# A decoder layer in one kernel: gates in column tiles, 1/rms columns by transfer, and three stretches in another order

## The chip, the core and the metric
The kernel runs on one core of a Trainium2 chip. The metric is the device time of one execution in microseconds (us). TensorE (PE) multiplies, VectorE (DVE), ScalarE (ACT) and GpSimd (POOL) work element by element, and SyncE (SP) issues most transfers. Each engine works through its own instructions in order and waits for others by semaphores.

## The reference
One step of a hybrid decoder layer for a prompt of 1024 tokens and 8 sequences of 8 new tokens, 1088 columns in all, in fp32:

```python
def rmsnorm(x, g):
    y = xf * lax.rsqrt(jnp.mean(xf * xf, axis=-1, keepdims=True) + EPS)
    return y * g

h = rmsnorm(x, pre_mix_g)
proj = h @ w_in               # 8 heads' q, k, v, output gate; 8 gate columns
i_pre, f_pre = gates          # + bias: 4 input and 4 forget gates
q_r, k_r = rotary(q_r, pos), rotary(k_r, pos) * scale
ret_out, S_new = retention_chunked(q_r, k_r, v_r, S_ret)            # 4 heads
ml_out, C, n, m = mlstm_chunked(q_m, k_m * scale, v_m, i_pre, f_pre, C, n, m)
ret_y = head_groupnorm(ret_out, ret_g) * silu(g_r)
ml_y = head_groupnorm(ml_out, ml_g) * sigmoid(o_m)
x = x + rmsnorm(concat([ret_y, ml_y]) @ w_out, post_mix_g)

up = rmsnorm(x, pre_ffn_g) @ w_up                # 1024 -> 2 x 2816
conv = causal depthwise convolution of width 3 over up, + conv_b
ffn = (gelu(gate) * value) @ w_down              # 2816 -> 1024
x = x + rmsnorm(ffn, post_ffn_g)
```

## The kernel before
Features lie on the 128 partitions and tokens on the free axis, in four blocks of 272 (`BLK`, `Q`). A large matmul is made of three fp32r products: each operand is split into a high part (a copy on ACT, L148) and a low part (a subtraction on DVE, L150), and `product` (L164) multiplies high by high, low by high and high by low. A projection (`proj`) loads and splits a weight of 128 columns and runs, block by block, 8 k-tiles x 3 products of 128x272; `proj`'s evacuation functions take each result from PSUM. What is multiplied there is x times the norm's gain; 1/rms of the token (`rb`, the same on all partitions) is multiplied in at the evacuation, for q and k of the retention heads through the rotation tables (L308).

The stages that the change touches:

- **Start of the mixer.** v of heads r0 and r1, then q of r0 with `pre_norm` in its middle, which sums squares on PE (`ssqb_pm`, L213) and forms `rb` block by block (L214 to L220), then k of r0. `token_norms` turns `rb` into columns (`rcol`, tokens on partitions) by matmuls with a column of the identity (L332). `gate_proj` projects the 8 gates: it splits the gates' weight and puts high and low side by side in 64 + 64 columns, so that each of the four blocks takes 8 x 2 matmuls (L359), evacuated by ACT and DVE. Four projections of output gates (12 to 15) follow, then head r0.
- **Gate tables.** `gate_consts` loads tables for the mLSTM heads (`xst`, from which DVE makes `upb` and `negsb`; `xsel`, which ACT copies to `sel`, L379). It stands behind head r0.
- **Heads.** `mix_head` goes through chunks of 128 tokens in pairs, `pair_of`, and the decode samples at last, `sample`. Every four chunks, and behind the sample, `finish` normalises the outputs on DVE (`on`, L687) and transposes them on PE (`yt`, L689) into `yT`. At a head's end two such `finish` are due: chunks 4 to 7 (four transposes) and the sample (one). The scheduler places their transposes among the matmuls of the next head's first projection.
- **FFN.** Of 22 pairs of up-projections (j), the first two (`PLAIN`) are multiplied directly and the others by a Strassen scheme with seven products on a pool of eight PSUM banks (psF); each product has two halves of 12 matmuls (L1088 to L1090), one bank each. Its operands T1 to T4 are differences of blocks of the input, split once. At the first Strassen pair (j = 2) there stand side by side: these splits, the weights' splits, the convolutions (`conv`, L1101 and L1103), gelu (L1107) and products (`pair_out`) of the plain pairs, and the evacuation of the first products: A11 by ACT (L1073), the others by DVE (L1062, L1066).

What sets the order is the order of the code, refined by a scheduler within each engine, and `tc.issue_after`, which holds an instruction back until a given one has been issued. PSUM pools have 2 banks (psA) and 6 banks (psB) in the mixer; a tile of a pool waits until the earlier tile in its place has been read.

## Time and profile before
| | before |
|---|---|
| time, median of 3 runs | 1339.77 us (1339.24 to 1342.83) |
| the profiled execution | 1338.16 us, of which the profile's span is 1336.4 us |
| mean granted clock of TensorE | 0.995 |
| PE busy | 1313.4 us, 98% of the span |
| DVE, ACT, POOL busy | 76%, 45%, 32% |

The profile is of one execution; "busy" excludes the issuing of transfers. The chain is followed back from the last instruction, each time to what released it. In it and in the rows of waits, a name such as `up_S` is a tile, and L1088 a line of the kernel. A matmul's own duration in the trace overlaps the next one's; what one costs is read from the distance of two starts, or from a piece of the chain.

### The profile page before, as it was taken

Reading aid. Unit: us, or ns where it says so; the run is one execution under the profiler, and the core shown is the slowest. Engines: PE = TensorE matmul, PEld = TensorE weight load, DVE = VectorE, ACT = ScalarE, POOL = GpSimd, SP = SyncE. Lnnn points to the kernel's source line nnn. Section 1 sums busy time; section 2 is a strip of 40 time slices with the busy share of each in tenths; the row PEclk is TensorE's granted clock in tenths of the full one; section 3 lists DMA queues with packets and bytes.
Section 4 is the critical chain, followed back from the end, with each engine's and each line's share of the span. In section 5 each row is a group of like instructions: output and inputs, shape, how many; then the busy total and the mean of one; then the engine's idle time right before and its main releaser. Section 6 shows DMA issues by size and latency. Waiting matters only on the chain.

```text
span 1336.4 us, 26898 instructions
## 1 busy us (share of the span) xinstructions
PE 1313.4 (98%) x10563; PEld 1301.6 (97%) x10563; DVE 1011.2 (76%) x2038; ACT 604.7 (45%) x1158; POOL 433.3 (32%) x565
## 2 busy tenths in 40 slices
PE   9999999999999999999989999999999999999996
PEld 9999999999999999999989999999999999999995
DVE  7877976558567467577899887877878788995677
ACT  7544433213324336455564443343434455463563
POOL 0344431589764000001144212222122214962002
PEclk9999999999999999999999999999999999999998
DMA  6433441576884214224034434433344359533363
GB/s 241 129 124 127 164 152 64 176 232 223 215 185 145 62 51 172 76 95 137 32 122 165 137 117 146 151 132 129 120 146 139 130 190 328 170 97 96 94 218 134
DMA packets 92734, 192.58 MB, mean 144 GB/s; under 512 B 16192, under 2 KB 41408, under 8 KB 92096
## 3 DMA queue, kind: packets, MB, share of 16 engines
q1 hardware_dynamic: 80304, 148.80, 33.6%
q0 software_dynamic: 12160, 41.95, 10.3%
q8 instruction: 83, 1.36, 0.4%
q14 instruction: 43, 0.35, 0.1%
q10 hardware_dynamic: 144, 0.11, 0.0%
HBM read 134.36 MB, written 56.47 MB: 143 GB/s over the span
## 4 chain that ended last, share of the span: by engine, by line
PE 92%; DVE 5%; ACT 1%; DMA 1%; issue 1%; SPq 0%; DVEq 0%; ACTq 0%
PE in L164 27%; PE out L164 7%; PE up_S L1090 6%; PE up_S L1088 6%; PE up_S L1089 6%; PE dn L1299 5%; PE dn L1300 5%; PE dn L1301 5%; PE up_A L1089 5%; PE up_A L1088 4%; PE up_A L1090 4%; PE up_A L1135 1%; PE up_A L1136 1%; PE up_A L1134 1%; PE gates L359 1%
## 5 line engine op out<-in xcount | busy, mean ns | idle before, releaser
L164 PE MATMUL in<-hh,wh_in 128*128 128x272 f32 x1024 | 297.8, 293 | 2.2 <-ACT wh_in L148 1.3
L164 PE MATMUL in<-hh,wl_in 128*128 128x272 f32 x1024 | 297.0, 292 | 0.0
L164 PE MATMUL in<-hl,wh_in 128*128 128x272 f32 x1024 | 296.9, 292 | 0.0
L164 PEld LDWEIGHTS in<-hh,wh_in 128*128 128x128 f32 x1024 | 192.4, 188 | 4.2 <-ACT wh_in L148 1.8
L164 PEld LDWEIGHTS in<-hl,wh_in 128*128 128x128 f32 x1024 | 192.0, 188 | 1.9 <-issue 1.7
L164 PEld LDWEIGHTS in<-hh,wl_in 128*128 128x128 f32 x1024 | 192.5, 189 | 0.1
L148 ACT ACTIVATE wh_up<-st_up 128x1024 fp32r<-128x1024 f32 x84 | 80.4, 959 | 163.4 <-PE up_S L1089 90.5
L150 DVE TENSOR_TENSOR wl_up<-st_up,wh_up 128x1024 fp32r<-128x1024 f32 x84 | 98.2, 1171 | 8.8 <-ACT wh_up L148 8.8
L1062 DVE TENSOR_TENSOR Uv<-Uv,up_S 128x272 f32<-128x272 f32 (+1 forms) x200 | 66.3, 375 | 46.1 <-PE up_S L1090 46.0
L1228 DVE TENSOR_TENSOR rb<-rb 128x544 fp32r<-128x544 f32 x78 | 75.0, 967 | 33.7 <-ACT rb L1227 33.3
L1227 ACT ACTIVATE rb<-rb 128x544 fp32r<-128x544 f32 x78 | 50.5, 650 | 77.2 <-DMA rb<-bd 65.3
L1248 POOL TENSOR_TENSOR wd<-wd 128x512 f32<-128x512 f32 x44 | 74.6, 1724 | 32.0 <-issue 12.7
L794 POOL TENSOR_TENSOR tab<-tab 128x256 f32<-128x256 f32 x104 | 80.5, 784 | 8.9 <-DMA tab<-in_wu 4.4
L1120 POOL TENSOR_TENSOR act<-act 128x544 f32<-128x544 f32 x40 | 64.4, 1610 | 57.6 <-DMA bd<-act 38.3
L1103 DVE SCALAR_TENSOR_TENSOR c<-Uv,vec,c 128x1024 f32<-128x1024 f32 (+1 forms) x88 | 69.0, 788 | 9.6 <-ACT c L1101 9.6
L1053 POOL MEMSET Ug<- 128x2 f32 x22 | 2.2, 100 | 217.2 <-DMA xr<-in_x 106.2
L1103 DVE SCALAR_TENSOR_TENSOR c<-Ug,vec,c 128x1024 f32<-128x1024 f32 x88 | 67.7, 805 | 0.0
L794 POOL TENSOR_TENSOR wq<-wq 128x256 f32<-128x256 f32 x56 | 49.7, 899 | 49.1 <-DMA wq<-in_wu 46.9
L1101 ACT ACTIVATE c<-Ug,vec 128x1024 f32<-128x1024 f32 (+1 forms) x44 | 34.6, 834 | 51.4 <-DVE Ug L1066 47.3
L794 POOL DMA_DIRECT2D tab<-in_wu x52 | 36.9, 715 | 51.4 <-DVE k_r L510 36.8
L150 DVE TENSOR_TENSOR wl_in<-st_in,wh_in 128x1024 fp32r<-128x1024 f32 (+2 forms) x33 | 40.7, 1233 | 13.8 <-ACT wh_in L148 13.8
L1088 PE MATMUL up_S<-B3h,wh_up 128*128 128x272 f32 x160 | 46.9, 293 | 3.7 <-ACT Uv L1073 3.7
(575 smaller groups left out, 4629.5 us busy)
## 6 DMA issues: line engine op xcount, KB each, us to landing
rb<-bd SPq DMA_DIRECT2D x76, 272.0 KB, 2.9
st_up<-sd SPq DMA_DIRECT2D x40, 512.0 KB, 3.8
bd<-act SPq DMA_DIRECT2D x33, 544.0 KB, 4.3
st_in<-in_wi SPq DMA_DIRECT2D x31, 512.0 KB, 4.4
tab<-in_wu POOLq DMA_DIRECT2D x52, 256.0 KB, 5.0
sd<-tab POOLq DMA_DIRECT2D x26, 512.0 KB, 3.9
st_up<-in_wu SPq DMA_DIRECT2D x24, 512.0 KB, 3.4
wd<-in_wd SPq DMA_DIRECT2D x44, 256.0 KB, 4.5
```

Of the source, the lines that this page charges most:

```text
L148: act = nc.scalar.activation(hi, x, AF.Copy)
L150: last["split"] = act, eng.tensor_tensor(lo, x, hi.bitcast(F32), ALU.subtract)
L164: nc.tensor.matmul(ps, u[:, k * P:(k + 1) * P], x[b // 2][k // 4][v][:, k % 4, qcols(b)], start=k == term == 0, stop=k == KT - 1 and term ...
L794: last["sums"] = f(*args)
L1088: nc.tensor.matmul(ps, wh[:, c], xh[:, k, n], start=k == 0, stop=False)
L1089: nc.tensor.matmul(ps, wh[:, c], xl[:, k, n], start=False, stop=False)
L1090: nc.tensor.matmul(ps, wl[:, c], xh[:, k, n], start=False, stop=k == 3)
L1103: nc.vector.scalar_tensor_tensor(c, u(i), cw(i), c, ALU.mult, ALU.add)
L1228: nc.vector.tensor_tensor(lo, x, hi.bitcast(F32), ALU.subtract)
L1248: nc.gpsimd.tensor_tensor(quad(p, out), quad(p, x), quad(p, y), op)
L1299: nc.tensor.matmul(t, wh[:, ms], ah, start=k == 0, stop=False)
L1300: nc.tensor.matmul(t, wh[:, ms], al, start=False, stop=False)
```

## The change
Five edits at once.

1. **Gates in column tiles.** The gates' weight is no longer split. DVE multiplies the eight used columns by the norm's gain in fp32; 32 fp32 matmuls with 32 columns each follow (8 k-tiles x 4 blocks, the blocks inside), each block into 32 partitions of its own in one bank. They multiply x itself (`xs`). Four DVE multiplies by `rb` evacuate the bank, and a transfer moves the input gates to their partitions.
2. **1/rms columns by transfers.** `token_norms` writes one row of `rb` to memory (`rbd`) and reads it back with tokens on partitions: one transfer for the eight chunks and four for the samples. The 9 matmuls (18 records, two passes each) go.
3. **Gate tables behind the gates.** `gate_consts` is called behind `gate_proj`, not behind head r0.
4. **Heads' ends.** A head's last two `finish` are kept in `held_back` and run in the next head's projections, with the transposes held back until k's block 3 (chunks 4 to 7) and v's block 0 (sample) have been issued.
5. **First Strassen pair.** T3's difference and splits now come before T1's, the convolutions of plain pair 0 wait for these splits, and gelu, products and the second plain pair's convolutions are issued behind product A11, with gelu held back until A11's evacuation (`last["evac"]`).

The order of PE's instructions at the gates, before (`in_3` is the last block of r0's k, `hh`, `hl` the high and low parts of the input):

```order
L164 MATMUL in_3_744<-hl_192,wh_in_647 128x272
L332 MATMUL rcol<-cst,rb 128x1 x2
L332 MATMUL rcol<-cst,sp_rb 128x1
L359 MATMUL gates_797<-hh_146,w_gates 128x272
L359 MATMUL gates_797<-hl_147,w_gates 128x272
```
And after (`in_1_887` is a block of projection 12, `x_102` to `x_105` the four token blocks of x):

```order
L164 MATMUL in_1_887<-hl_149,wh_in_854 128x272
L356 MATMUL gates<-x_102,st_gates 32x272
L356 MATMUL gates<-x_103,st_gates 32x272
L356 MATMUL gates<-x_104,st_gates 32x272
L356 MATMUL gates<-x_105,st_gates 32x272
```
Neighbours now belong to different blocks, and 18 matmuls of projection 12 stand ahead of the gates, between and behind the blocks of k.

ACT's order ahead of the gates, before (`sw_kr` are the swapped halves of k's blocks; `in_1`, `in_2` their banks):

```order
L508 ACTIVATE sw_kr_707<-in_1_682 64x272
L509 ACTIVATE sw_kr_707<-in_1_682 64x272
L508 ACTIVATE sw_kr_738<-in_2_713 64x272
L509 ACTIVATE sw_kr_738<-in_2_713 64x272
L508 ACTIVATE sw_kr_769<-in_3_744 64x272
```
And after:

```order
L509 ACTIVATE sw_kr_708<-in_1_683 64x272
L510 ACTIVATE sw_kr_708<-in_1_683 64x272
L380 ACTIVATE sel<-xsel 100x1024
L509 ACTIVATE sw_kr_739<-in_2_714 64x272
L510 ACTIVATE sw_kr_739<-in_2_714 64x272
```
The copy of `sel` stands ahead of block 2's swaps. On DVE the gain multiplies (L352), `upb` and `negsb` stand right behind the first block's L215, and on SP the load of `xsel` stands behind `rbd`, which reads the finished `rb`.

PE's order at the end of head m0, before (`on_m`, `on_m0s`: the head's normalised outputs; `in_3`: a block of the next head's first projection):

```order
L689 MATMUL yt_m_4219<-cst,on_m_4064 128x128
L164 MATMUL in_3_4457<-hh_189,wl_in_4376 128x272
L689 MATMUL yt_m_4219<-cst,on_m_4064 128x128
L164 MATMUL in_3_4457<-hl_190,wh_in_4375 128x272
L164 MATMUL in_3_4457<-hh_191,wh_in_4375 128x272
```
The other two transposes of `yt_m` stand just ahead of these rows, and `yt_m0s` follows five matmuls behind the last one shown. And after (`in_3_4348` is k's block 3, `in_0_4409` v's block 0):

```order
L164 MATMUL in_3_4348<-hh_191,wh_in_4266 128x272
L164 MATMUL in_3_4348<-hh_191,wl_in_4267 128x272
L164 MATMUL in_3_4348<-hl_192,wh_in_4266 128x272
L699 MATMUL yt_m_4393<-cst,on_m_4007 128x128 x4
L164 MATMUL in_0_4409<-hh_146,wh_in_4405 128x272
```
The four transposes stand together behind k's last block; `yt_m0s` stands behind v's four blocks, 96 matmuls later.

ACT's order at the first Strassen pair, before (`Uv<-up_A` on L1073: A11's two banks):

```order
L148 ACTIVATE wh_up_0_8586<-st_up_0_8584 128x1024
L148 ACTIVATE wh_up_1_8649<-st_up_1_8647 128x1024
L1107 ACT_TABLE_LOAD
L1107 ACTIVATE c_8504<-c_8504 128x1088
L1073 ACTIVATE Uv_8577<-up_A_8426 128x272
L1073 ACTIVATE Uv_8577<-up_A_8439 128x272
```
And after:

```order
L148 ACTIVATE wh_up_0_8529<-st_up_0_8527 128x1024
L1086 ACTIVATE Uv_8492<-up_A_8369 128x272
L1086 ACTIVATE Uv_8492<-up_A_8382 128x272
L1119 ACT_TABLE_LOAD
L1119 ACTIVATE c_8453<-c_8453 128x1088
L148 ACTIVATE wh_up_1_8592<-st_up_1_8590 128x1024
```
A11's evacuation moved ahead of the table load, the gelu and a weight's copy. On DVE, T3's splits moved ahead of T1's, and the next weight's second split behind A12's evacuation and `act`.

The diff:

```diff
@@ -161 +161 @@
     def product(ps, w, x, b, k, term):
 
         u, v = ((w[0], 0), (w[1], 0), (w[0], 1))[term]
-        nc.tensor.matmul(ps, u[:, k * P:(k + 1) * P], x[b // 2][k // 4][v][:, k % 4, qcols(b)],
-                         start=k == term == 0, stop=k == KT - 1 and term == 2)
+        last["product", b] = nc.tensor.matmul(ps, u[:, k * P:(k + 1) * P], x[b // 2][k // 4][v][:, k % 4, qcols(b)],
+                                              start=k == term == 0, stop=k == KT - 1 and term == 2)
 
     def dense(ps, w, x, b):
 
@@ -325 +325 @@
     def spread_tile(name):
         return m2.tile([P, NB * 129], F32, tag="vx", bufs=1, name=name)
 
+    rbd = dr.tile([1, T], F32, name="rbd")
+
     def token_norms():
-        ps = bank(psB, 9, "rcol")
-        rs = spread_copy(rb, spread_tile("sp_rb")[:, :P])
-        for c in range(9):
-            nc.tensor.matmul(ps[:, c:c + 1], chunk(rb, c) if c < 8 else rs, ident[:, 0:1], start=True, stop=True)
-        nc.vector.tensor_copy(rcol, ps)
+        nc.sync.dma_start(rbd, rb[0:1, :])
+        nc.sync.dma_start(rcol[:, :NCH], rbd[0, :LP].rearrange("(c p) -> p c", p=P))
+        for g in range(G):
+            nc.sync.dma_start(rcol[GW * g:GW * (g + 1), NCH:], rbd[0, LP - LEAD + TS // G * g:][:GW].unsqueeze(1))
 
 
     idb = mp.tile([P, P], BF16, name="idb")
@@ -345 +346 @@
     gates = []
 
     def gate_proj():
-        fg = yT[3][32:32 + NH, 0, :]
-        ig = yT[3][:NH, 0, :]
+        w = stage_w(a["wg"], "gates").rearrange("p (k c) -> p k c", k=KT)
+        gain = vec[:, V_PREMIX:V_PREMIX + KT].unsqueeze(2).broadcast_to([P, KT, NH])
+        for c in range(2):
+            nc.vector.tensor_tensor(w[:, :, NH * c:NH * (c + 1)], w[:, :, 32 * c:32 * c + NH], gain, ALU.mult)
+        ps = bank(psA, Q, "gates")
+        for k in range(KT):
+            for b in range(4):
+                nc.tensor.matmul(ps[GW * b:GW * (b + 1), :], w[:, k, :GW], xs[b][:, k, :],
+                                 start=k == 0, stop=k == KT - 1)
+        yT.extend(flat("yT", i, k=2) for i in range(4))
+        both = yT[3][:2 * NH, 0, :]
+        fg, ig = yT[3][:NH, 0, :], yT[3][32:32 + NH, 0, :]
         gates.extend([fg, ig])
-        st = stage_w(a["wg"], "gates").rearrange("p (k c) -> p k c", k=KT)
-        w = wp.tile([P, D], F32R, tag="whi", name="w_gates").rearrange("p (k c) -> p k c", k=KT)
-        split_to(st[:, :, :64], w[:, :, :64], w[:, :, 64:])
         for b in range(4):
             o0, n = BLK[b]
-            ps = bank(psA, n, f"gates{b}")
-            for k in range(KT):
-                for i, x in enumerate(h[b // 2][k // 4]):
-                    nc.tensor.matmul(ps, w[:, k, :], x[:, k % 4, qcols(b)], start=k == i == 0,
-                                     stop=k == KT - 1 and i == 1)
-            gs = m2.tile([P, Q], F32, tag="sw", name=f"gs{b}")[:64, :n]
-            nc.scalar.activation(gs, ps[64:, :], AF.Copy)
-            nc.vector.tensor_tensor(gs, gs, ps[:64, :], ALU.add)
-            nc.vector.tensor_tensor(fg[:, o0:o0 + n], gs[0:NH, :], rb[0:NH, o0:o0 + n], ALU.mult)
-            nc.vector.tensor_tensor(ig[:, o0:o0 + n], gs[32:32 + NH, :], rb[32:32 + NH, o0:o0 + n], ALU.mult)
+            own = slice(GW * b, GW * b + 2 * NH)
+            nc.vector.tensor_tensor(both[:, o0:o0 + n], ps[own, :], rb[own, o0:o0 + n], ALU.mult)
+        nc.sync.dma_start(ig, yT[3][NH:2 * NH, 0, :])
         nc.scalar.activation(fg, fg, AF.Identity, bias=vec[0:NH, V_BG:V_BG + 1])
         nc.scalar.activation(ig, ig, AF.Identity, bias=vec[0:NH, V_BG + 1:V_BG + 2])
 
@@ -538 +539 @@
 
     EARLY = (0, 1, 2, 3)
     turns = {"wq": 0}
-    early = []
+    early, held_back = [], []
+
+    def finish_previous(n, b):
+        for _ in range(min(n, len(held_back))):
+            held_back.pop(0)(last["product", b])
 
     def mix_head(hd, ml):
 
@@ -555 +560 @@
         if ml:
             proj((16 + hd, evac_norm(q, 1.0)))
             proj((20 + hd, evac_norm(k, SCALE)))
+            finish_previous(1, 3)
             proj((24 + hd, evac_copy(v)))
+            finish_previous(1, 0)
         else:
             eq, ek = evac_rot(q, f"q{nm}"), evac_rot(k, f"k{nm}")
             if hd == 0:
@@ -564 +571 @@
             else:
                 proj((hd, eq))
                 proj((NH + hd, ek))
+                finish_previous(1 if hd > 1 else 2, 3)
             if hd == 0:
                 token_norms()
-                yT.extend(flat("yT", i, k=2) for i in range(4))
             if hd > 1:
                 proj((2 * NH + hd, evac_copy(v)))
+                finish_previous(1, 0)
             if hd == 0:
                 gate_proj()
+                gate_consts()
                 for _ in range(5):
                     next(rows)
                 for i in range(NH):
@@ -662 +671 @@
...
-        def finish(on, mv, c0, L, name):
+        def finish(on, mv, c0, L, name, after=None):
 
             sh = [P, L]
             small = lambda tag: m2.tile([P, 4], F32, tag=tag, name=f"{tag}_{name}")[:, :L]
@@ -686 +695 @@
             for i in range(L):
                 nc.vector.tensor_scalar(on[:, i, :P], on[:, i, :P], mv[:, i, 0:1], A[:, i:i + 1],
                                         ALU.subtract, ALU.mult)
-                nc.tensor.transpose(ps[:, i * P:(i + 1) * P], on[:, i, :P], ident)
+                with tc.issue_after(after.ins) if after else nullcontext():
+                    nc.tensor.transpose(ps[:, i * P:(i + 1) * P], on[:, i, :P], ident)
             y = yT[hid // 2][:, hid % 2, c0 * CH:c0 * CH + L * P if c0 < 8 else T]
...
@@ -728 +738 @@
             nc.sync.dma_start(o["cs" if ml else "ss"][hd].rearrange("p (s v) -> p s v", s=NB), sb[:, :, :P])
...
-            return lambda: finish(on, mv, 8, 1, f"{nm}s")
+            return lambda after=None: finish(on, mv, 8, 1, f"{nm}s", after)
 
         S = None
         g = math.exp(CH * LG[hd])
@@ -761 +771 @@
                 S = S2
             stats(on, po, c0 % 4, 2, mv, f"{nm}{c0}")
             if c0 % 4 == 2:
-                return lambda: finish(on, mv, c0 - 2, 4, f"{nm}{c0}")
+                return lambda after=None: finish(on, mv, c0 - 2, 4, f"{nm}{c0}", after)
 
         todo = None
         order = [[0, 1], [2, 3], [4, 5], [6, 7], [8]]
@@ -769 +779 @@
         for i, cs in enumerate(order):
             cur, ready = ready, front(order[i + 1]) if i + 1 < len(order) else None
             done = sample(*cur) if cs == [8] else pair_of(cs[0], *cur)
-            if todo:
+            if todo and i + 1 == len(order) and hid + 1 < 2 * NH:
+                held_back.append(todo)
+            elif todo:
                 todo()
             todo = done
             next(rows, None)
             if hid > 2 or i % 2 == 0:
                 next(wsums, None)
         nc.sync.dma_start(o["cp" if ml else "sp"][hd], S)
-        todo()
+        if hid + 1 < 2 * NH:
+            held_back.append(todo)
+        else:
+            todo()
 
 
     sd = dr.tile([JT, P, 4, D // 2], F32, name="sd")
@@ -824 +839 @@
     rows = gate_rows()
     for hd in range(NH):
         mix_head(hd, False)
-        if hd == 0:
-            gate_consts()
...
@@ -1070 +1083 @@
...
-            "A11": ("B1", lambda i, ps: nc.scalar.activation(first(i), ps, AF.Copy)),
+            "A11": ("B1", lambda i, ps: last.update(evac=nc.scalar.activation(first(i), ps, AF.Copy))),
...
@@ -1100 +1113 @@
         for c, u in ((C[:, :LP], lambda i: U[:, i:i + LP]), (seq(C[:, LP:]), lambda i: own[:, :, i:i + LS])):
             nc.scalar.activation(c, u(2), AF.Identity, scale=cw(2), bias=vec[:, V_CB + jt:V_CB + jt + 1])
             for i in (1, 0):
-                nc.vector.scalar_tensor_tensor(c, u(i), cw(i), c, ALU.mult, ALU.add)
+                last["conv"] = nc.vector.scalar_tensor_tensor(c, u(i), cw(i), c, ALU.mult, ALU.add)
+
+    def gelu():
+        last["gelu"] = nc.scalar.activation(cs_[:, 0, :], cs_[:, 0, :], AF.Gelu_apprx_tanh)
 
     def convs(j, ug, uv):
         conv(ug, cs_[:, 0, :], j)
-        last["gelu"] = nc.scalar.activation(cs_[:, 0, :], cs_[:, 0, :], AF.Gelu_apprx_tanh)
+        gelu()
         conv(uv, cs_[:, 1, :], JT + j)
 
     def pair_out(j):
@@ -1173 +1189 @@
             split(name, i, sums[name][:, :, qcols(i)])
 
     difference("T2", 4)
+    last["sq"], last["acc"] = last["split"]
+    difference("T3", 6)
+    last["sq"], last["acc"] = last["split"]
     difference("T1", 10)
     last["sq"], last["acc"] = last["split"]
     next(prep)
     cs_ = flat("c", 3, k=2)
-    convs(0, *firsts[0][2])
-    difference("T3", 6)
+    for c, u in enumerate(firsts[0][2]):
+        conv(u, cs_[:, c, :], JT * c)
+    last["acc"] = last["conv"]
     for _ in prep:
         pass
     X["T4"] = [bigp.tile([P, 4, 2 * Q], F32R, tag=f"f{i}", name=f"T4{'hl'[i]}") for i in range(2)]
     for i in range(2):
         split("T4", i, mo[1][0][:, :, qcols(i)])
     acts_ = flat("act", 2, k=2)
-    for j, _, rows in firsts:
-        if j:
-            convs(j, *rows)
-        pair_out(j)
+
+    def finish_plain():
+        with tc.issue_after(last["evac"].ins):
+            gelu()
+        pair_out(0)
+        convs(1, *firsts[1][2])
+        pair_out(1)
+
     for j in range(PLAIN, JT):
         ws = nxt
         prep = weight_prep(j + 1) if j + 1 < JT else iter(())
@@ -1199 +1223 @@
             for name in names:
                 for i in range(2):
                     (held.pop(0) if held else product(name, i))()
+                if j == PLAIN and name == "A11":
+                    finish_plain()
             nxt = next(prep, None) or nxt
         convs(j, ug, uv)
         pair_out(j)
```

## The prediction
> **What bounds the kernel now.** I read the page's busy times and its chain first, then PE's waits, then chain, timelines and clock around each wait that the change touches.
>
> ```profile
> PE 1313.4 (98%) x10563; PEld 1301.6 (97%) x10563; DVE 1011.2 (76%) x2038; ACT 604.7 (45%) x1158; POOL 433.3 (32%) x565
> PE 92%; DVE 5%; ACT 1%; DMA 1%; issue 1%; SPq 0%; DVEq 0%; ACTq 0%
> ```
> PE is busy for 98% of the span and carries 92% of the chain that ended last. Time is won by issuing less to PE or by taking one of its few stalls away. Of the view of PE's waits three rows bear on the change (who waited for whom; us in total, times, longest):
>
> ```profile
> PE up_S L1088 <- ACT Uv L1073: 3.7, 1, 3.7
> ...
> PE in L164 <- DVE k_r L510: 0.9, 1, 0.9
> ...
> PE yt_m L689 <- DVE on_m L687: 0.7, 3, 0.3
> ```
>
> **Gates and 1/rms columns.** The chain near the start (start, us, what):
>
> ```profile
> 34.42 0.46 PE ssqb_pm L213 x2
> ...
> 54.23 1.23 PE rcol L332 x12
> 55.46 6.15 PE in L164 x48
> 61.61 0.56 PE rcol L332 x6
> 62.17 4.12 PE gates L359 x32
> 66.29 1.63 PE in L164 x13
> 67.92 4.01 PE gates L359 x32
> ```
> Before, the gates are 64 matmuls of 272 columns: 4.12 + 4.01 = 8.1 us. After, they are 32 fp32 matmuls, each on 32 of the array's 128 columns. What an fp32 matmul of 272 columns costs shows ssqb_pm: two passes (x2), 0.46 us. One behind the other, 32 of them cost 32 x 0.46 = 14.7 us; four neighbours side by side, 8 x 0.46 = 3.7 us. The order puts the four token blocks inside the loop over k, so neighbours sit on different column tiles. Which price holds, the decode samples' product tells; it has the same tiling:
>
> ```profile
> 328.89 0.65 PE L706 MATMUL o_m<-sb_m,qx 128*32 128x129 f32 x16
> 329.46 0.72 PE L717 MATMUL us_m<-sp_m,kz_m 32*128 32x258 f32 x8
> ```
> These 16 records are 8 fp32 matmuls on 32 columns, two passes each; from their start to the next instruction's it is 329.46 - 328.89 = 0.57 us. A pass of 272 columns is 0.23 us, so one of 129 should be 0.23 x 129/272 = 0.109: 16 in a row would need 1.74 us, four at a time 0.44. The group is near the second, with 0.13 left for the change of tiling. Each tile there reads its own moving data and loads its own weights, as the gates' tiles will. I take 3.7 + 0.1 = 3.8 us: **-4.3 us** (ends: -4.5, and +6.6 without overlap).
>
> The Trainium skill, "TensorE: Matmul & The Clock Gate", Part 3: Packing small matmuls, reports 2.38x for three column tiles, a share of 0.79 of the full factor. By that the gates would take an estimated 3.7/0.79 = 4.7 us, and the sum would be 0.9 us higher. The trace's own factor is 1.74/0.57 = 3.05 of four, about that share, but over a stretch so short that the switch of tiling weighs in it.
>
> The 18 rcol records leave PE: 1.23 + 0.56 = **-1.8 us**. In their place SP's queue gets one transfer of rb to memory and five of 4-byte elements back. The nearest row (last column: us from issue to landing):
>
> ```profile
> sb_m<-in_sn SPq DMA_DIRECT2D x4, 4.0 KB, 5.8
> ```
> Two such steps take some 12 us; rcol's first reader is head r0's front, behind the gates and four output-gate projections (4 x 96 matmuls of 0.128 = 49 us). Head r0's state and the following weight loads stand behind them in the queue, under the same cover. I cost them at nothing (ends 0 and +2); without the cover, r0's front would wait.
> The gates' evacuation (four DVE multiplies on 8 partitions for four ACT copies and twelve DVE operations) lies beside PE's projections: nothing.
>
> **Gate tables.** Before, they are loaded behind head r0 and stop DVE, then PE:
>
> ```profile
> 147.99 3.08 DMA xst<-in_cx
> ...
> 151.09 0.75 DVE upb L375
> ```
> ```profile
> 151.91 0.29 PE L164 MATMUL in<-hl,wh_in 128*128 128x272 f32 x1
> 153.06 0.39 PE L164 MATMUL in<-hh,wh_in 128*128 128x272 f32 x1 [0.86 <-DVE k_r L510]
> ```
> From 151.91 to 153.06 it is 1.15 us where 0.13 is usual: **-1.0 us** (other end 0, if DVE is late there anyway). Now the new place. ACT's copy to sel waited long for its transfer, and DVE's rows of the start say when the tables would come:
>
> ```profile
> 157.00 1.06 ACT L379 ACTIVATE sel<-xsel 100x1024 fp32r<-100x1024 f32 x1 [3.69 <-DMA xsel<-in_cx]
> ```
> ```profile
> 35.27 0.36 SPq L136 DMA_DIRECT2D st_gates<-in_wg  x1
> ```
> ```profile
> 38.46 0.43 DVE L215 TENSOR_SCALAR rb<-ssqb_pm 128x272 f32<-128x272 f32 x1
> ...
> 46.29 0.44 DVE L218 SCALAR_TENSOR_TENSOR sums_sb<-sums_sb,rb 128x272 f32<-128x272 f32 x1 [0.68 <-ACT sums_sb L217]
> ...
> 52.47 0.44 DVE L220 SCALAR_TENSOR_TENSOR rb<-sums_sb 128x272 f32<-128x272 f32 x1
> ```
> ```profile
> 58.63 0.40 ACT L508 ACTIVATE sw_kr<-in 64x272 f32<-64x272 f32 x1 [2.22 <-PE in L164]
> ```
> Behind the first L215 (38.46), DVE now needs st_gates, issued at 35.27, and xst, issued behind it (3.1 us): it goes on at about 40.3 instead of 38.8, 1.5 late. Of that, 0.7 goes into the idle time at 46.29; PE's banks are ahead there, nothing lost. The last block's 1/rms (52.47) then comes 0.8 later, and about 1.3 more since proj 12's weight split and two k_r operations now stand ahead of it: 54.5, done 54.9. SP waits for it with rbd, then issues xsel: 55.5, landed 3.6 later at 59.1. ACT copies sel (1.06) to 60.2, and only then does the swaps of k's block 2, which stood at 58.63; with these (0.8) and DVE's read (0.4), k's bank is free at 61.4. The gates need it at 62.17 - 1.8 (rcol) + 18 x 0.128 (matmuls of projection 12 that now stand ahead) = 62.7. So 1.3 us are left: **0** (ends 0 and +2).
>
> **Heads' ends.** The transposes that wait at the ends of m0 and m1:
>
> ```profile
> 337.37 0.33 PE L689 MATMUL yt_m<-cst,on_m 128*128 128x128 f32 x1 [0.32 <-DVE on_m L687]
> ...
> 339.10 0.30 PE L689 MATMUL yt_m0s<-cst,on_m0s 128*128 128x128 f32 x1 [0.29 <-DVE on_m0s L687]
> ```
> ```profile
> 389.24 0.30 PE L689 MATMUL yt_m1s<-cst,on_m1s 128*128 128x128 f32 x1 [0.42 <-DVE on_m1s L687]
> ```
> 0.32 + 0.29 + 0.42 = 1.03 us idle, and 0.16 each for the start after it (k_r's stall: 1.02 lost, 0.86 of it idle): **-1.5 us** (other end 0). The change holds the transposes back by at least a projection (24 matmuls, 3 us, or more), over twice the longest wait. The other two waits of yt_m (0.7 in all) are inside a head, and stay. What is late next: yT, which only the output projection reads, far later.
>
> **First Strassen pair.**
>
> ```profile
> 673.67 0.29 PE L1090 MATMUL up_S<-T1h,wl_up 128*128 128x272 f32 x1
> 677.69 0.39 PE L1088 MATMUL up_S<-B3h,wh_up 128*128 128x272 f32 x1 [3.73 <-ACT Uv L1073]
> ```
> ```profile
> 673.87 1.06 ACT wh_up L148
> 674.95 1.28 ACT L1107
> ...
> 677.26 0.39 ACT Uv L1073
> ```
> ```profile
> 677.69:681.65 3.96, 3.96 (x20) 0.58 0.46 133
> 681.65:685.60 3.95, 3.95 (x33) 0.99 0.53 202
> ```
> PE has filled its banks and waits for ACT to empty A11's, behind a weight's copy, a table load and the gelu: 677.69 - 673.67 - 0.13 = 3.9 us. Then the granted clock (fourth number of a window; ahead of it length, busy time, records) is 0.58 for 4 us: 20 matmuls where the next window has 33, 13 x 0.128 = 1.7 us. In the new order these two evacuations stand ahead of table load and gelu, right behind the first weight's copy, so they can run before 673.67. That takes away 5.6. But then PE comes earlier to the banks that DVE empties:
>
> ```profile
> 661.67 2.49 DVE L150 TENSOR_TENSOR T1l<-mo,T1h 128x1088 fp32r<-128x1088 f32 x2 [2.42 <-ACT T1h L148]
> ```
> ```profile
> 679.60 0.78 DVE L1062 TENSOR_TENSOR Ug<-Uv,up_A 128x272 f32<-128x272 f32 x2
> ```
> DVE is busy from 661.67 to past 679.60; the change only moves one weight split (1.2) behind A12's evacuation and can fill the 2.42 of idle time: 679.60 - 3.6 = 676.0. A11's two banks keep PE going for 24 x 0.126 = 3.0 us, from 673.8 to 676.8: in time. S2's come next, behind act (1.2) and that split (1.2): 676.7 + 2.4 + 0.35 = 679.5, PE there at 679.8. Behind them conv operations of 1.2 us each now stand between the evacuations, at 1.5 us of PE a bank; I allow 1.2 us of new waits: **-4.4 us** (ends -5.6, and -2.5 where DVE gains none of its idle time).
>
> **The sum.** -4.3 - 1.8 - 1.0 + 0 - 1.5 - 4.4 = -13.0. The profiled execution took 1338.16 us (span 1336.4 and 1.8 around it), so 1325.2; the median, 1339.77, is 1.6 above that execution: **1326.8 us**. What a measurement can tell from no change is about 0.3%, 4 us.
>
> **Rivals.**
> - *Column tiles run one behind the other.* Gates 14.7 instead of 3.8 us: 1326.8 + 10.9 = 1337.7, no change. For it: 272 columns of four moving streams are more than L706 ever reads at once. Against it: 0.57 us for 16 passes.
> - *DVE takes over the Strassen wait.* If DVE is not earlier at A12's banks than 679.60 less the one split, PE waits from 676.8 to 678.8, then at S2 and S1 again: about 4 of the 5.6 us come back; 1330 us. For it: DVE has no idle time from 661.67 on. Against it: 2.42 us just ahead.
> - *Stalls only move* (k_r's and the heads' 2.5 us turn up elsewhere): 1329.3 us. For it: DVE's order at the heads' ends is the same. Against it: the wait is PE's, and PE has other work.
> - *Slower: the gates wait for sel.* ACT stands at sel until xsel lands, and k's evacuation, PE's bank and the gates wait behind it. Past 1.3 us each us costs one; an idle time like the 3.9 us at 673.67 brings the half clock with 1.7 more. To lose what the rest wins and 4 us more, xsel must land 1.3 + 13.0 + 4.0 - 1.7 = 16.6 us later than I put it, at about 75.7: over 1344 us. For it: five more transfers crowd SP's queue. Against it: xsel is issued ahead of them, and 16 us is four times any landing here.
>
> The Trainium skill, same page, Part 1: The HAM clock gate, says that an idle window of about 3.4 us halves TensorE's clock, and about as much busy time brings it back. The trace agrees: 0.58 behind 3.9 us of idle time, for one window.
>
> **Chances.** Forecast as summed (1323 to 1329): 0.60. DVE's wait: 0.17. Stalls that move: 0.10. No overlap: 0.08. Gates behind sel: 0.05, most of that a few us that end above my forecast or at no change, 0.02 slower; 0.02 more for slower by what I don't see. Faster 0.87, same 0.09, slower 0.04. The range: low end where the pair wins all (-1.2), rounds and neighbours give some more, 1322; high end where DVE's wait and moved stalls come together, 1333. The no-overlap and the slower case stay outside.
>
> **What would show it.** Gates: 64 records within 4 us, no rcol on PE. No wait of PE for k_r near 150 and for on_m0s, on_m1s. In the pair no wait for ACT Uv over 1 us, and no window at half clock; small waits for DVE Ug or Uv in its place. DVE's first L215 followed by an idle time of 1 to 2 us, sel ended near 60, gates started near 61 to 62. Wrong if the gates' matmuls start 0.1 us apart or more on average, if PE waits over 3 us ahead of them, or if a new stall of DVE at 676 to 682 is over 3 us.

## The result, and the profile after

| | before | after |
|---|---|---|
| median of 4 runs | 1339.51 us (1339.11 to 1342.83) | 1329.84 us (1327.90 to 1331.05) |
| ratio to before, 95% interval | | 0.9921 [0.9900, 0.9942] |
| profiled execution (span) | 1338.16 us (1336.4) | 1330.78 us (1329.0) |

The change made the kernel 9.7 us faster; 13.0 were forecast, and the range held the time. Between the two profiled executions it is 7.4 us, since the one of before lies 1.4 under its median and the one of after 0.9 over. The traces speak of these 7.4 us. One of k_first's five executions, further down, took 1408.58 us at a granted clock of 0.849; its time there is the median of the other four.

The gates, in PE's timeline (start, us, instruction, count; in brackets, where there are any, the idle time ahead and what ended it):

```profile
62.47 0.29 PE L164 MATMUL in<-hl,wh_in 128*128 128x272 f32 x1
62.89 3.87 PE L356 MATMUL gates<-x,st_gates 128*32 128x272 f32 x64
66.69 0.39 PE L164 MATMUL in<-hh,wh_in 128*128 128x272 f32 x1
```
The 64 passes take 66.69 - 62.89 = 3.80 us, as forecast (8.13 before). The distance ahead of them is 0.42 instead of 0.13: 0.3 us of wait for k's bank. Four rows of PE's waits now, in the same view as before (who waited for whom; us in total, times, longest):

```profile
PE in L164 <- DVE k_m L502: 1.5, 2, 0.8
PE up_S L1101 <- ACT Uv L1086: 1.3, 1, 1.3
...
PE in L164 <- DVE z L521: 0.9, 2, 0.6
...
PE in L164 <- DVE k_r L511: 0.2, 1, 0.2
```
The 3.7 us at the Strassen start are 1.3 now, one pair later; k_r's 0.9 are 0.2. No wait for a transpose's input is left in the view. But two rows are new: k_m stands where the transposes of the heads' ends were, with more idle time than they had (1.03), and PE had no wait for z in the output-gate projections before. Each new row is two waits:

```profile
90.30 0.39 PE L164 MATMUL in<-hh,wh_in 128*128 128x272 f32 x1 [0.34 <-DVE z L521]
96.02 0.39 PE L164 MATMUL in<-hh,wh_in 128*128 128x272 f32 x1 [0.56 <-DVE z L521]
336.30 0.39 PE L164 MATMUL in<-hh,wh_in 128*128 128x272 f32 x1 [0.85 <-DVE k_m L502]
386.00 0.39 PE L164 MATMUL in<-hh,wh_in 128*128 128x272 f32 x1 [0.61 <-DVE k_m L502]
```
The wait that is left in the Strassen stage, on ACT and on PE:

```profile
685.71 1.06 ACT L148 ACTIVATE wh_up<-st_up 128x1024 fp32r<-128x1024 f32 x1 [1.90 <-PE up_A L1102]
686.67 0.67 ACT L1086 ACTIVATE Uv<-up_A 128x272 f32<-128x272 f32 x2
```
```profile
687.10 0.39 PE L1101 MATMUL up_S<-T2h,wh_up 128*128 128x272 f32 x1 [1.31 <-ACT Uv L1086]
```
The windows around it (length, PE busy and records, granted clock, DMA share, GB/s) have no half clock left:

```profile
672.00:676.00 4.00, 3.86 (x31) 1.00 0.55 198
676.00:680.00 4.00, 4.00 (x34) 1.00 0.54 181
...
684.00:687.10 3.10, 1.79 (x15) 1.00 0.50 163
```

### The profile page after: what moved, and what is told of

Read it like the earlier page. It is cut to its first block, busy times and chain, and to the rows that moved or that the text cites. A ratio compares the mean times of both kernels' runs of the same rounds, so it can differ in the third digit from the quotient of the medians.

```text
span 1329.0 us, 26853 instructions
## 1 busy us (share of the span) xinstructions
PE 1308.0 (98%) x10545; PEld 1292.7 (97%) x10545; DVE 1008.0 (76%) x2030; ACT 602.5 (45%) x1152; POOL 439.7 (33%) x565
## 4 chain that ended last, share of the span: by engine, by line
PE 83%; DVE 6%; ACT 2%; issue 1%; DMA 1%; DVEq 0%; ACTq 0%
PE in L164 21%; PE out L164 7%; PE up_S L1103 6%; PE up_S L1101 6%; PE up_S L1102 6%; PE dn L1325 5%; PE dn L1326 5%; PE dn L1327 4%; PE up_A L1102 4%; PE up_A L1101 4%; PE up_A L1103 4%; PE up_A L1151 1%; PE up_A L1152 1%; PE up_A L1150 1%; DVE facc L1407 1%
## 5 line engine op out<-in xcount | busy, mean ns | idle before, releaser
L150 DVE TENSOR_TENSOR wl_up<-st_up,wh_up 128x1024 fp32r<-128x1024 f32 x84 | 95.3, 1137 | 9.1 <-ACT wh_up L148 9.1
L809 POOL TENSOR_TENSOR tab<-tab 128x256 f32<-128x256 f32 x104 | 85.1, 829 | 10.5 <-DMA tab<-in_wu 6.0
L1274 POOL TENSOR_TENSOR wd<-wd 128x512 f32<-128x512 f32 x44 | 77.7, 1795 | 28.3 <-issue 13.0
L148 ACT ACTIVATE wh_in<-st_in 128x1024 fp32r<-128x1024 f32 (+2 forms) x33 | 34.0, 1029 | 33.4 <-PE in L164 30.0
```

What stands on the lines that cost most here:

```text
L148: act = nc.scalar.activation(hi, x, AF.Copy)
L150: last["split"] = act, eng.tensor_tensor(lo, x, hi.bitcast(F32), ALU.subtract)
L809: last["sums"] = f(*args)
L1274: nc.gpsimd.tensor_tensor(quad(p, out), quad(p, x), quad(p, y), op)
```

## The experiments

**One edit at a time, on the kernel before.** Each kernel has one of the five edits of the change as its diff shows them, the other four undone. Time of before beside them: 1339.57 us (1339.48 beside rcol_only and tables_only).

| kernel | median | ratio to before |
|---|---|---|
| gates_only | 1337.40 us | 0.9982 [0.9969, 0.9995] |
| rcol_only | 1338.33 us | 0.9991 [0.9982, 1.0000] |
| tables_only | 1339.58 us | 1.0002 [0.9993, 1.0011] |
| heads_only | 1340.30 us | 1.0004 [0.9990, 1.0017] |
| pair_only | 1335.78 us | 0.9973 [0.9960, 0.9986] |

> The kernel before with the first edit alone (gates in fp32 column tiles, input gates moved by a transfer). Theory: the 64 passes of the gates take 3.8 us instead of 8.1, wherever the rest stands: 4.3 us less there. The wait of PE for z (0.9 us in the trace of after) comes from this edit too, since ACT stands at the input gates' bias until their transfer has landed and the sums of the gates behind it come late: then 3.1 to 3.6 us faster than before, with PE waiting for DVE z between 85 and 105 us. Rival: the wait for z comes from the other edits (PE arrives earlier): 4.3 us faster and no wait for z.

```diff
...
+        for k in range(KT):
+            for b in range(4):
+                nc.tensor.matmul(ps[GW * b:GW * (b + 1), :], w[:, k, :GW], xs[b][:, k, :],
+                                 start=k == 0, stop=k == KT - 1)
...
+        nc.sync.dma_start(ig, yT[3][NH:2 * NH, 0, :])
...
```
```profile
62.06 3.88 PE L355 MATMUL gates<-x,st_gates 128*32 128x272 f32 x64
65.87 0.39 PE L164 MATMUL in<-hh,wh_in 128*128 128x272 f32 x1
```
```profile
108.87 0.39 PE L164 MATMUL in<-hh,wh_in 128*128 128x272 f32 x1 [0.47 <-DVE z L520]
```
The gates take 3.81 us here too. A wait for z comes with this edit alone, shorter than in after (0.5 instead of 0.9) and later than the theory put it. The theory holds in kind; of 4.3 us won 2.2 are left in the median, less than the 3.1 to 3.6 expected.

Its trace also shows that the price of the first Strassen pair had been read from one execution. The stall of 3.9 us at the Strassen start is still in this kernel, at 673.21, and the half clock behind it lasts longer than in the trace of before, where the two windows showed 0.58 and 0.99:

```profile
673.21:677.21 4.00, 4.00 (x17) 0.50 0.46 135
677.21:681.21 4.00, 4.00 (x28) 0.82 0.52 197
```
From the first product of that Strassen pair to the first of the next, PE takes 27.48 us here and 26.57 in before. The kernels with this stall fall into two groups: before and tables_only (26.59) with the shorter half clock, gates_only, rcol_only (27.55) and heads_only (27.30) with the longer. So what the same stall costs differs by 0.7 to 1.0 us between executions.

> The kernel before with the second edit alone (1/rms columns by transfers). Theory: 18 records leave PE, 1.8 us; the transfers are hidden behind the gates and four projections: 1.8 us faster than before, no PE wait for rcol's readers (vts) in head r0. Rival: what PE gains is lost at the next wait for DVE (k_r near 151 us grows from 0.9 us), since DVE's work is not shorter: 0 to 0.9 us faster.

```diff
-            nc.tensor.matmul(ps[:, c:c + 1], chunk(rb, c) if c < 8 else rs, ident[:, 0:1], ...)
+        nc.sync.dma_start(rbd, rb[0:1, :])
+        nc.sync.dma_start(rcol[:, :NCH], rbd[0, :LP].rearrange("(c p) -> p c", p=P))
...
```
1.2 us faster; PE's wait for k_r is 1.0 (0.9 before), and no wait for rcol's readers is in its view. Between the theory's 1.8 and the rival's 0.9, with an interval that holds both.

> The kernel before with the third edit alone (gate tables behind the gates instead of behind head r0). Theory: the wait of PE for k_r near 151 us (0.9 idle, 1.0 lost) goes and nothing takes its place: 1.0 us faster than before. Rival: DVE is late there for the other work at the end of head r0 too, the wait only shrinks or moves to the transposes of r0's sample: 0 to 0.4 us faster.

```diff
                 gate_proj()
+                gate_consts()
...
-        if hd == 0:
-            gate_consts()
```
```profile
156.21 0.30 PE L690 MATMUL yt_r0s<-cst,on_r0s 128*128 128x128 f32 x1 [0.36 <-DVE on_r0s L688]
```
No wait for k_r, but this one for the transpose of r0's sample, 4 us later, and no gain that can be measured: the rival's account.

> The kernel before with the fourth edit alone (the last transposes of a head held back into the next head's projections). Theory: DVE, not the place of the transposes, is late at a head's end; PE then waits for the evacuation of k (k_m) that stands behind on_m in DVE's order: within 0.5 us of the time before, no wait for on_m0s and on_m1s, in their place waits for k_m of 0.7 to 1.5 us in all. Rival (the prediction): 1.5 us faster, no new wait.

```diff
+            if todo and i + 1 == len(order) and hid + 1 < 2 * NH:
+                held_back.append(todo)
...
+            finish_previous(1, 3)
```
The trace is against my theory: PE waits neither for transposes nor for k_m at the ends of m0 and m1. Yet the median is no better than before's. The profiled execution, 1337.84 us, is the fastest of twelve and 2.5 us under their median, so its trace can't explain that median. What it does show is that other waits came: 0.6 us for r0's sample (yt_r0s) where k_r's 0.9 is gone, dn on facc 1.5 us instead of 0.7, and the longer half clock. DVE's order at the heads' ends is that of after. What differs is how long DVE takes. On_m of m0 and m1, first after, then heads_only:

```profile
332.03 1.53 DVE L696 TENSOR_SCALAR on_m<-on_m,mv_m,A_m 128x128 f32<-128x128 f32 x4
382.34 2.41 DVE L696 TENSOR_SCALAR on_m<-on_m,mv_m,A_m 128x128 f32<-128x128 f32 x4
```
```profile
335.68 1.12 DVE L695 TENSOR_SCALAR on_m<-on_m,mv_m,A_m 128x128 f32<-128x128 f32 x4
384.17 1.16 DVE L695 TENSOR_SCALAR on_m<-on_m,mv_m,A_m 128x128 f32<-128x128 f32 x4
```
And POOL beside m1's in after, and beside m0's in heads_only:

```profile
381.33 3.08 POOL L809 TENSOR_TENSOR tab<-tab 128x256 f32<-128x256 f32 x4
384.71 0.75 POOL L809 DMA_DIRECT2D sd<-tab  x1 [0.30 <-POOL tab L809]
```
```profile
332.37 3.06 POOL L808 TENSOR_TENSOR tab<-tab 128x256 f32<-128x256 f32 x4 [0.63 <-DMA tab<-in_wu]
336.74 0.75 POOL L808 DMA_DIRECT2D sd<-tab  x1 [1.31 <-issue]
```
In after POOL adds from 381.33 to 384.4 and on_m of m1, which falls into it, takes 2.41 us; in heads_only POOL stops at 335.43, ahead of on_m. The trace of after has 72 such DVE operations (128x128, one chunk each). The 42 with nothing on POOL beside them have a median of 0.342 us, the 19 that overlap a TENSOR_TENSOR of POOL one of 0.772. The other 11, beside POOL's issuing of transfers only, have a median of 0.347, but the longest takes 0.845. On_m of m0 in after is such a case for the most part: POOL issues transfers until 333.3 and adds from 333.35 on, where the small operations between on_m and k_m stand.

The Trainium skill, "SBUF — State Buffer", Who interferes with whom, says that DVE's tensor_scalar can take the ports that DVE shares with GpSimd, and that whichever comes second then waits for the other's whole instruction. The trace agrees: one POOL addition is 0.75 us, and a DVE operation beside one may double.

> The changed kernel without the additions on POOL that form the Strassen sums of the weights (four TENSOR_TENSOR for each part; the transfers stay, so the up-projection works on sums that are not made). Theory: DVE's small operations at the heads' ends take longer when POOL adds beside them; without that, the four on_m take 1.1 to 1.2 us at the ends of both m0 and m1 (1.5 and 2.4 in the trace of after), and PE's waits for k_m there fall from 1.5 us to under 0.4: 1.5 to 3 us faster than the changed kernel. Rival: what DVE does there is slow by itself or by its own waits: on_m stays at 1.5 us or more in one of the two places, k_m's waits at 1 us or more.

```diff
-                for o_, x, y, op in ((a21, a11, a21, ALU.subtract), ...):
-                    queued(nc.gpsimd.tensor_tensor, o_, x, y, op)
```
```profile
331.12 1.12 DVE L696 TENSOR_SCALAR on_m<-on_m,mv_m,A_m 128x128 f32<-128x128 f32 x4
379.84 1.12 DVE L696 TENSOR_SCALAR on_m<-on_m,mv_m,A_m 128x128 f32<-128x128 f32 x4
```
The kernel leaves out POOL's additions, and so what it computes is not the layer. On_m takes 1.12 us in both places, and the waits for k_m are gone: the theory's part on POOL and DVE holds. The time does not: 1329.86 us, ratio 0.9924 [0.9909, 0.9939], as after. PE waits 0.9 us for `hh` near 8 us, which it did not in after, and z's wait grew from 0.9 to 2.1 us, because POOL, which stood longer at transfers, cleared the gate rows' tile late (ACT, start 74.96; 70.54 in after):

```profile
74.96 1.11 ACT L403 ACTIVATE yT<-yT 4x1088 f32<-4x1088 f32 x1 [4.99 <-POOL yT L400]
```

> The kernel before with the fifth edit alone (order at the first Strassen pair). Theory: 3.9 us of idle time and 1.7 us of half clock go, and 1.3 to 1.5 us come back one pair later, where ACT stands at a weight's copy that waits for PE ahead of A11's evacuation: 3.5 to 4.3 us faster than before, no half clock near 680. Rival: the wait one pair later comes from the five edits together: 5.0 to 5.6 us faster.

```diff
+    difference("T3", 6)
     difference("T1", 10)
...
+                if j == PLAIN and name == "A11":
+                    finish_plain()
```
3.8 us faster. PE waits 1.3 us for ACT Uv one pair later, as in after, and the clock is full behind it. The theory holds: the remaining wait belongs to this edit and not to the others.

**Do tiles overlap in any order?**

> The changed kernel with the gates' two loops exchanged: the eight k-tiles of a block follow one another on the same column tile, and only then comes the next block. Theory: only neighbours on different tiles run side by side, so the 64 passes now take 64 x 0.23 = 14.7 us instead of 3.8: 10 to 11 us slower than the changed kernel, about 1340. Rival: PE overlaps tiles whatever their order within some window of instructions: the gates stay under 6 us and the time within 2 us of the changed kernel's.

```diff
-        for k in range(KT):
-            for b in range(4):
+        for b in range(4):
+            for k in range(KT):
```
```profile
62.78 12.19 PE L356 MATMUL gates<-x,st_gates 128*32 128x272 f32 x64
74.91 0.39 PE L164 MATMUL in<-hh,wh_in 128*128 128x272 f32 x1
```
12.1 us instead of 3.80, in all 7.1 us slower than after (1336.97 us, ratio to before 0.9981 [0.9968, 0.9994]). Two passes on one tile start 0.229 us apart; in after, four on different tiles start within 0.02 us. It is less than the 14.7 expected because at each change of block some passes of the next tile started 5 or 30 ns behind the last ones of the old tile. So tiles run side by side where they are close in the order. PE's loss at the gates is 8.3 us and the time's is 7.1: PE has no wait for z here, while its waits for k_m are 2.0 us (1.5 in after).

**Three mends on the changed kernel, and all of them.** Time of before beside them: 1339.35 us (1339.48 beside the last).

| kernel | median | ratio to before |
|---|---|---|
| after | 1329.84 us | 0.9921 [0.9900, 0.9942] |
| k_first | 1327.89 us | 0.9911 [0.9895, 0.9926] |
| ig_later | 1328.65 us | 0.9913 [0.9898, 0.9928] |
| evac_first | 1329.10 us | 0.9917 [0.9903, 0.9931] |
| all_three | 1327.47 us | 0.9909 [0.9891, 0.9927] |
| all_and_conv | 1326.26 us | 0.9904 [0.9890, 0.9918] |

> The changed kernel with on_m and on_m0s (the last normalisations of a head, on DVE) held back behind the evacuation of block 2 of the next head's k. Theory: PE waits at the ends of m0 and m1 for k's bank, since on_m stands ahead of k_m in DVE's order, and takes longer whenever POOL adds weights beside it; with k_m first the waits for k_m (1.5 us of idle time, 1.8 lost) go: 1.5 to 1.8 us faster than the changed kernel, no wait for k_m. Rival: DVE as a whole is late at a head's end, and PE waits as long for the transposes (yt_m) or for the next k_m: within 0.5 us of the changed kernel.

```diff
+            last["norm", b] = nc.vector.scalar_tensor_tensor(t[:, o0:o0 + n], ps, scale, ...)
...
+                with tc.issue_after(last["norm", 2].ins) if after and ("norm", 2) in last else nullcontext():
                     nc.vector.tensor_scalar(on[:, i, :P], ...)
```
1.95 us less than after, near the 1.5 to 1.8 expected, though the intervals overlap. Its waits are read from all_three and all_and_conv, which contain the edit. Neither waits for k_m, although on_m takes 2.9 us at the end of m0 in both, longer than in after. In its place both wait 0.4 us in all for the transposes (yt_m): a part of what the rival said.

> The changed kernel with the input gates' bias on ACT behind the forget gates' exponentials, so that ACT no longer stands at the transfer of the input gates. Theory: the wait for that transfer holds up the gate rows on ACT and DVE, and these come between PE's output-gate projections and DVE's z: without it DVE's first gate row starts 2 to 2.5 us sooner after the gates, the waits for z (0.9 us idle, 1.2 lost) go, 1.0 to 1.2 us faster than the changed kernel. Rival: the waits come from the long DVE rows themselves (a scan of 2.4 us, sums of 1.3), which stand ahead of z in DVE's order: the rows start sooner, PE waits as before, within 0.5 us.

```diff
-        nc.scalar.activation(ig, ig, AF.Identity, bias=vec[0:NH, V_BG + 1:V_BG + 2])
...
         aa = rst
+        with tc.issue_after(last["rows"].ins):
+            nc.scalar.activation(ig, ig, AF.Identity, bias=vec[0:NH, V_BG + 1:V_BG + 2])
```
DVE's first gate row in after, and in ig_later:

```profile
75.53 0.89 DVE L406 TENSOR_SCALAR yT<-yT 4x1088 f32<-4x1088 f32 x1 [4.31 <-ACT yT L404]
```
```profile
72.42 0.71 DVE L405 TENSOR_SCALAR yT<-yT 4x1088 f32<-4x1088 f32 x1 [1.16 <-ACT yT L403]
```
3.1 us sooner, and PE no longer waits for the z of the output-gate projections; the time is 1.2 us less than after's, as expected, with overlapping intervals. In after, ACT stood until 73.08 at a transfer issued at 68.66:

```profile
68.66 0.75 SPq L366 DMA_DIRECT2D yT<-yT  x1
```
```profile
73.08 1.21 ACT L368 ACTIVATE yT<-yT,vec 4x1088 f32<-4x1088 f32 x1 [1.43 <-DMA yT<-yT]
```
The theory holds: the wait for z comes from what ACT stands at ahead of DVE's rows, in after the input gates' transfer, and not from the length of DVE's rows. How long that is differs: from issue to the bias it was 4.4 us in after, 6.0 in evac_first, 4.0 in gates_only and 3.6 in tiles_in_turn, and PE waited for z 0.9, 1.5, 0.5 and 0 us in all. In no_weight_sums it was POOL's clearing instead.

> The changed kernel with the first weight copy of the pair after next (wh_up_0 of j = 4) held back behind A11's evacuation of pair j = 3. Theory: the 1.3 us that PE waits for ACT near 686 come from this copy alone, which waits for PE to give its tile free: 1.3 to 1.5 us faster than the changed kernel, no wait of PE for ACT Uv. Rival: DVE, which empties S2's banks just then, is as late, and PE waits for DVE Uv instead: within 0.5 us of the changed kernel.

```diff
+            held = (last["evac"], None) if i == 0 and j == PLAIN + 2 else None
+            split_to(x, hi, lo, nc.vector, (last["sq"], last["acc"]) if i in (1, 2) or j == 1 else held)
```
```profile
684.99 0.69 ACT L1087 ACTIVATE Uv<-up_A 128x272 f32<-128x272 f32 x2 [2.51 <-DVE c L1117]
```
My theory falls. The copy is out of the way, and ACT waits for DVE instead: the last convolution of the second plain pair reads the tile that A11 is to be put into. PE's wait fell from 1.3 to 1.0 us only, and the time by 0.7 us.
This run shows something else. Up to the Strassen stage its instructions have the same order as after's on all engines. Yet on_m took 1.12 and 1.61 us in it, PE never waited for k_m, and it waited 1.5 us for z. So these waits differ between executions of one order of instructions, by how POOL's and the transfers' work falls against DVE's.

> The three edits of the runs beside it together, on the changed kernel. Theory: they are at three places far apart and add up: 3.8 to 4.5 us faster than the changed kernel, about 1325.5. Rival: each shifts POOL's and DVE's work against PE's further on, and new waits eat half of it: 1327 to 1328.

2.4 us less than after, where the theory had 3.8 to 4.5: the rival's range. It contains evac_first's edit, which brings little.

> The three edits of all_three, and two weight splits of pair j = 3 on DVE (wl_up_2, wl_up_3) held back behind the last convolution of the second plain pair. Theory: PE's last wait at the Strassen start (1.0 us for ACT Uv near 683) comes from DVE: that convolution (683.4 to 684.9 in the trace of evac_first) reads the tile into which A11 of j = 3 is evacuated, and 1.8 us of splits stand ahead of it. With the splits behind it, 1.0 to 1.3 us less than all_three: about 1326.3, and no wait for ACT Uv. Rival: DVE is the bound of this stretch; PE waits as long for another evacuation or split a few us later: within 0.4 us of all_three, 1327.5.

```diff
+            held = ((last["evac"], None) if i == 0 and j == PLAIN + 2 else
+                    (None, last["conv"]) if i > 1 and j == PLAIN + 1 else None)
...
```
PE's longest waits in its trace:

```profile
PE ssqb_fin L213 <- DVE facc_sq L1347: 2.2, 1, 2.2
PE in L164 <- ACT wh_in L148: 1.3, 1, 1.3
PE warm L159 <- DVE ones L203: 1.1, 1, 1.1
PE out L164 <- DVE z L536: 1.0, 1, 1.0
PE dn L1331 <- DVE facc L1358: 0.8, 2, 0.4
PE yt_m L702 <- DVE on_m L699: 0.4, 2, 0.2
```
No wait for ACT Uv, k_m or those projections' z is left, though on_m took 2.86 us at the end of m0 here. 1326.26 us is 1.2 under all_three and 3.6 under after, as the theory had it: the wait at the Strassen start was DVE's order. From the first product of the second Strassen pair to the first of the third, PE takes 21.28 us here and 22.48 in all_three, 1.2 less; the pair behind it, which waits for nothing, takes 21.06. The interval of the ratio overlaps after's, but all four times (1325.71 to 1327.82 us) lie under the four of after (1327.90 to 1331.05).

## Why the prediction was right, and where not

- **Gates, -4.3 us**: right. 3.80 us in the trace, and tiles_in_turn shows that the four tiles must follow one another for it. The Trainium skill's share of 0.79 ("TensorE: Matmul & The Clock Gate", Part 3: Packing small matmuls) would have made an estimated 4.7 us of it; this run has 14.7/3.80 = 3.9 of four.
- **"The gates' evacuation lies beside PE's projections: nothing"**: wrong. I named the work that covered it and left out what its transfer holds up. It lands 4.4 us after its issue; ACT stands at it in order, gate rows behind ACT, and z behind the gate rows in DVE's order. Lost: 0.50 + 0.72 = 1.2 us of PE's starts in after, where starts are 0.62 and 0.85 us apart instead of 0.13. ig_later shows the cause.
- **rcol, -1.8**: the records are gone, their transfers hidden; alone it brought 1.2.
- **Gate tables, -1.0**: 0.7 in after (0.2 us idle and 0.2 for the start are left). Alone nothing is left of it: the bound that I gave as "0, if DVE is late there anyway" was the value for the edit alone. At the new place the chain was as worked out: xsel issued at 55.68 (55.5 forecast), landed 1.4 us later than put, sel copied from 60.48, gates started at 62.89 with 0.3 us of wait. The slower rival had its place right; 1.3 us of slack were just used up. Against that rival I wrote that 16 us is four times any landing; the row that I had quoted has 5.8 us, so it is under three times.
- **Heads' ends, -1.5**: wrong in sign, and the largest miss of the sum: +0.5 in after, where the waits for k_m cost 1.0 + 0.3 us of starts at m0 and 0.8 at m1, in the place of the transposes' 1.5. The transposes no longer wait, but k's bank stands behind on_m in DVE's order; that, I had not asked. The rival "stalls only move" had it. How much moves differs: PE waits for k_m 0 us in heads_only, evac_first and no_weight_sums, 1.2 in ig_later and 2.0 in tiles_in_turn. no_weight_sums shows that DVE's operations are long there because of POOL's additions; that the waits go with them rests on one execution, and two with the additions had none either. Why the additions fall on DVE's operations in one execution and not in another is not shown.
- **First pair, -4.4**: -3.3. From the first product of the first Strassen pair to the first of the third, PE took 47.65 us in before and 44.33 in after. A pair without waits takes 21.06, so 5.5 us of stall and half clock went (5.6 forecast), and 0.4 in the first pair and 1.8 in the second came back, where I had allowed 1.2. The reason is the one given, DVE's conv operations, but I had put the new waits at S2's banks; the one that counted came one pair later, at the tile of A11. Against an execution with the longer half clock the same edit wins up to 1.0 more; that pair_only's median has 3.8 fits both kinds, but how often each comes was not counted.
- **Chances**: "DVE's wait" had 0.17 and "stalls that move" 0.10. Both came true in part; with the wait for z, which no rival had, they put the time 3 us above the forecast. The range was set wide enough for these two rivals together. That the wait for z fitted in as well is luck.

The five kernels with one edit sum to 0.48% (0.18 + 0.09 - 0.02 - 0.04 + 0.27), the change to 0.79%. With half-widths of 0.09 to 0.14% for each the difference isn't shown to be real, and what the edits do to each other stays open.

In after's trace the terms sum to -4.3 - 1.8 + 0.3 (the gates' wait) + 1.2 (z) - 0.7 + 0.5 - 3.3 = -8.1 us; the spans differ by 7.4. The other 0.7 lie in pieces of under 1 us, both ways, that no run followed; 0.3 of it is there before the gates, and the two waits of yt_m inside head m1, which were to stay, are gone.

## What to carry to other kernels

A transfer put in the place of arithmetic is priced by the first instruction that waits for it in order, and by everything behind that one on its engine, even if its result is needed much later. When a wait of the bounding engine is moved, look at which bank or tile that engine needs next, and what stands ahead of its evacuation. Where DVE's small operations end on the path, their time beside GpSimd's work is the one to reckon with, and one profile shows only one way in which the two fall together. The same goes for what a stall costs in half clock.

## What the runs showed that was not expected

A DVE tensor_scalar of 128x128 takes 0.342 us alone and a median of 0.77 beside a POOL addition, and the same order of instructions had waits for k_m of 1.5 us in one execution and none in another. Behind the same stall of 3.9 us, the two windows of 4 us showed granted clocks of 0.58 and 0.99 in one execution (before) and 0.50 and 0.82 in another (gates_only). Four fp32 column tiles of 272 columns start 5 to 8 ns apart and together cost one pass (0.23 us).
